# A convolution's pair sums put between the scans and the next gates, and the start of the recurrence gate written in another order

## The chip, the cores and the metric

The kernel runs on one core of a Trainium2 chip. The metric is the device time of one execution in microseconds (us), the median of three runs. Five engines work side by side, each through a queue of its own in a fixed order: TensorE (PE, matmuls), VectorE (DVE), ScalarE (ACT), GpSimd (POOL) and SyncE (SP, which here issues DMA transfers). An instruction waits until what it reads is written and what it overwrites has been read.

## The reference, cut to what matters

Two layers over 1024 latent tokens of 1024 channels (and 256 context tokens that feed the recurrence alone). The change lies in the first layer:

```python
z = h @ p["w_in"]
va, vg, ga, xb, gb = jnp.split(z, [...], axis=-1)
# branch A: 31 taps along the tokens, then layernorm
u = va * jax.nn.sigmoid(vg)
u = depthwise_conv(u, p["conv_w"], p["conv_b"], CONV_PAD)
y_a = jax.nn.silu(layernorm(u, p["ln_g"], p["ln_b"])) * jax.nn.silu(ga)
# branch B: a gated linear recurrence, forwards and backwards
a, bx = lru_coeffs(u2, p)         # u2: 4 taps over xb; sigmoid gates from 128 x 128 blocks
y_b = (scan forwards + scan backwards) * jax.nn.silu(gb)
x = x + gate[:, None] * (jnp.concatenate([y_a, y_b], axis=-1) @ p["w_out"])
```

Everything is float32. A product is formed in three matmuls (high by high, high by low, low by high) from operands that are split into a high part (a cast, names ending in h) and the remainder (a subtraction, names ending in l).

## The kernel before

Channels lie on the 128 partitions, so that a tile holds 128 channels and 1024 tokens, and each of the first layer's products is done in 8 column blocks j. A loop of **8 rounds** (L661 to L740) goes through the blocks. In round j, PE forms vg, va, the context's and the latents' xb of the next block, and the gates of this block, 12 groups of three matmuls dealt out between those of xb (`gate_steps`, L630). ACT turns the gate groups into sigmoids; POOL subtracts the low parts of the weights (`wl_vg`, `wl_va`, `wl_xb`) and multiplies the recurrence's inputs (`rec_input`, `rec_scaled`: tiles `l` with `uc`, and `l` with `l`); DVE does the four taps (`uc`), the products va by sigmoid (`u`), and for the block before it the two directions' scans (`rec_scan`, L610) and their sum (`rec_sum`, L624: tile `l`, 128 x 1024, both operands in SBUF).

The 31-tap convolution (`conv`, L509) is a stream of small DVE steps that `fill(n)` draws into the other work, n steps at a time: the numbers of `fill` set how far each conv has come at each place. It works on even and odd tokens apart: one sum over even taps, one over odd taps, and one of both phases' sum with summed taps, from which the others are subtracted. That sum is formed in place, odd tokens plus even tokens (L528, tile `u`, two SBUF operands). Most steps accumulate in PSUM (tile `conv`) and so have one SBUF operand. At a conv's end, L547 adds its result to the layernorm's sum (`lnsum`).

In the rounds and up to L926 the helpers `on`, `act`, `cast`, `gp`, `vec` (L441 to L497) hold each engine to the order of the code. `fixed[0] = False` (L928) frees DVE's; from there a scheduler orders the work.

The gate of branch B is multiplied in a loop after the rounds (L910): for each block, the weights of a gb product, the product, its silu (`sb`), and `yr` (the scans' sum, read back from DRAM, times the silu) with its split (`ybh`, `ybl`). The products `wob` of L951 read these. The layernorm follows on its sum: `mu` (L936) is a matmul with ones over `lnsum`, and the products `ga` (L995) wait in PSUM until the normalised `u` is multiplied in (L1001).

The eight gate columns of the modulation (L655, a sum over a product of a loaded tile `l` with the condition's tile `cL`) stand ahead of the rounds; `cL` isn't used afterwards.

Of the kernel before, what the change touches and what calls it, by code (L numbers as in the profile page):

```python
# [55 lines left out]
def body(ctx, tc, xT, ctxT, cc, ccol, modT, modW, win, gw, wout, wu, grp, wg, wo1, small, edge, ident, outT):  # L56
# [443 lines left out]
    def tap(acc_, src, w, o, last_=False):  # L500
        a, b = max(0, -o), H - max(0, o)
        vec(nc.vector.scalar_tensor_tensor, out=(src if last_ else acc_)[:, a:b], in0=src[:, a + o : b + o],
            scalar=w, in1=acc_[:, a:b], op0=mult, op1=add)
        if last_:
            vec(nc.vector.tensor_copy, out=src[:, b:], in_=acc_[:, b:])
# [3 lines left out]
    def conv(j):  # L509
        acc_, late = banks(f"conv{j}", 0)  # L510
        ue, uo = us[j][:, 0::2], us[j][:, 1::2]
        bias, edge_ = col(O_CONVB + j), edges[:, j : j + 1]
# [17 lines left out]
        tap(acc_, ue, w(2 * NT - 1), NT - 1 - 7, True)  # L530
        yield
        vec(nc.vector.scalar_tensor_tensor, out=acc_, in0=uo, scalar=both(7), in1=ue, op0=mult, op1=sub)
# [3 lines left out]
        vec(nc.vector.scalar_tensor_tensor, out=late[:, : H - 1], in0=uo[:, 1:], scalar=both(8), in1=late[:, 1:],  # L536
            op0=mult, op1=sub)
        vec(nc.vector.tensor_copy, out=late[:, H - 1 :], in_=edge_)
        yield
        for i, n in enumerate([n for n in range(NT) if n not in (7, 8)]):  # L540
            tap((acc_, late)[i % 2], uo, both(n), n - 7)
            yield
        tap(acc_, uo, both(NT), NT - 7, True)
# [3 lines left out]
        for h in range(2):  # L547
            if j > 0:
                first = us[0][:, HALF[h]] if j == 1 else lnacc[h][:, :H]
                vec(nc.vector.tensor_tensor, out=lnacc[h][:, :H], in0=first, in1=us[j][:, HALF[h]], op=add)  # L550
                yield
# [15 lines left out]
    with ExitStack() as actx:  # L567
# [87 lines left out]
        for m in range(2 * KT, 3 * KT):  # L655
            raw = L[m % 6][:, :D]
            nc.sync.dma_start(raw, modT[0, m])
            mod_tile(m0, 0, m, raw, (cL,), raw)

        state, free = None, [L[0], L[1], L[2], L[3], L[4], L[5]]  # L660
        for j in range(KT):  # L661
# [15 lines left out]
            if state is None:  # L677
                act(sg[1], vg[1], AF.Sigmoid)
            uh, ul = utile(f"uh{j}", F32R), utile(f"ul{j}", F32R)
            cast(uh, uc)  # L680
            if state is not None:
                act(sg[1], vg[1], AF.Sigmoid)
# [48 lines left out]
            for n, _ in enumerate(gate_steps(j, (gwh, gwl), (uh, ul), gates)):  # L731
# [3 lines left out]
                if n == 7:  # L735
# [3 lines left out]
            fill(5)  # L739
# [12 lines left out]
        def gb_product(j, w):  # L752
            gps[j] = [psum(f"gb{j}_{h}") for h in range(2)]
# [156 lines left out]
    for j in range(1, KT + 1):  # L910
        if 1 < j < KT:
            gb_silu(j)
        gb_weights(j + 2)
        if j + 2 < KT:
            gb_product(j + 2, gws[j + 2])
        n = j - 1
        th, tl = d2tile(f"ybh{n}", F32R), d2tile(f"ybl{n}", F32R)
        for h in range(2):
# [5 lines left out]
            fill(6)  # L924
        bh.append(th)
        bl.append(tl)  # L926

    fixed[0] = False  # L928
    all_of(going[0])
    for j in range(begun[0], KT):  # L930
        all_of(conv(j))

# [662 lines left out]
```

## Time and profile before

| | |
|---|---|
| median of 3 runs (lowest, highest) | 1392.46 us (1392.46, 1395.89) |
| the profiled execution's own time | 1395.02 us |
| its span, first to last instruction | 1393.2 us |
| mean granted TensorE clock | 0.971 |
| busy DVE, ACT, POOL | 1204.9, 627.7, 353.0 us |

The span is what one execution's instructions take; the run's own time has 1.8 us around it. A busy share is an average over stages with different limits. The stages of interest lie between 100 and 700 us: the modulation's gate columns and the first round (to 150), the rounds (to 467), the recurrence gate's products (to 582), the `wob` products (to 657), and the layernorm with the `ga` products. Times in rows count from the span's start. In a row of the timeline stand the start, the length, engine, line, operation, names (output, arrow, inputs), shapes, a count, and in brackets the idle time of the engine before it with what ended it.

### The profile page before, as it was taken

Reading aid. Unit: us, or ns where it says so; the run is one execution under the profiler, and the core shown is the slowest. Engines: PE = TensorE matmul, PEld = TensorE weight load, DVE = VectorE, ACT = ScalarE, POOL = GpSimd, SP = SyncE. Lnnn points to the kernel's source line nnn. Section 1 sums busy time; section 2 is a strip of 40 time slices with the busy share of each in tenths; the row PEclk is TensorE's granted clock in tenths of the full one; section 3 lists DMA queues with packets and bytes.
Section 4 is the critical chain, followed back from the end, with each engine's and each line's share of the span. In section 5 each row is a group of like instructions: output and inputs, shape, how many; then the busy total and the mean of one; then the engine's idle time right before and its main releaser. Section 6 shows DMA issues by size and latency. Waiting matters only on the chain. (4 is left out here: it accounts for less than half of the span.)

```text
span 1393.2 us, 15819 instructions
## 1 busy us (share of the span) xinstructions
PE 1293.3 (93%) x5664; PEld 1046.3 (75%) x5664; DVE 1204.9 (86%) x1790; ACT 627.7 (45%) x902; POOL 353.0 (25%) x172
## 2 busy tenths in 40 slices
PE   7888999999899959899699999999999999899896
PEld 5467887887787848688488788788878888778684
DVE  7986699999999999988887884999989986876775
ACT  6352656664556613201643544753333434534442
POOL 5182454464536525412411004100000000000002
PEclk9999999999999989999899999999999999999998
DMA  9744111111112122253244635523334324757633
GB/s 349 279 136 159 38 45 39 69 68 38 61 53 69 46 76 98 96 177 129 75 151 139 211 132 198 169 70 136 133 124 137 121 97 145 242 187 265 231 110 121
DMA packets 82866, 181.79 MB, mean 130 GB/s; under 512 B 7778, under 2 KB 27618, under 8 KB 82788
## 3 DMA queue, kind: packets, MB, share of 16 engines
q1 hardware_dynamic: 74340, 176.60, 36.7%
q10 hardware_dynamic: 8448, 4.20, 1.0%
q8 instruction: 44, 0.72, 0.2%
q14 instruction: 34, 0.28, 0.1%
HBM read 136.72 MB, written 44.04 MB: 130 GB/s over the span
## 5 line engine op out<-in xcount | busy, mean ns | idle before, releaser
L445 DVE SCALAR_TENSOR_TENSOR conv<-u,sm,conv 128x505 f32<-128x505 f32 (+6 forms) x196 | 134.1, 742 | 0.8
L1415 POOL TENSOR_TENSOR o<-x,rr 128x256 f32<-128x256 f32 (+1 forms) x9 | 8.0, 930 | 462.6 <-ACT rr L1403 460.0
L445 ACT ACTIVATE l<-g,sm 128x512 f32<-128x512 f32 (+1 forms) x96 | 58.0, 617 | 79.0 <-PE g L445 59.6
L103 POOL TENSOR_TENSOR wl_wu<-wr_wu,wh_wu 128x1024 fp32r<-128x1024 f32 x16 | 39.8, 2491 | 153.6 <-ACT wh_wu L102 148.1
L133 PE MATMUL ga<-h0h,wh_ga 128*128 128x512 f32 x128 | 50.9, 398 | 13.5 <-DVE u L1001 13.5
L445 PE MATMUL gb<-h0h,wh_gb 128*128 128x512 f32 x128 | 51.0, 399 | 12.1 <-ACT wh_gb L445 12.1
L445 POOL TENSOR_TENSOR l<-l,uc 128x1280 f32<-128x1280 f32 x16 | 61.9, 3891 | 0.0
L445 DVE SCALAR_TENSOR_TENSOR conv<-u,wsum,conv 128x506 f32<-128x506 f32 (+3 forms) x88 | 60.2, 743 | 0.2
L445 DVE TENSOR_TENSOR_SCAN l<-l,l 128x256 f32<-128x256 f32 (+1 forms) x32 | 56.5, 1767 | 1.1
L256 PE MATMUL fold<-gh,wh_wu 128*128 128x512 f32 x128 | 52.8, 414 | 3.1 <-ACT wh_wu L102 3.1
L257 PE MATMUL fold<-gl,wh_wu 128*128 128x512 f32 x128 | 52.1, 407 | 3.7 <-DVE gl L103 3.7
L445 POOL TENSOR_TENSOR l<-l,l 128x1280 f32<-128x1280 f32 x16 | 47.8, 3010 | 27.0 <-ACT l L445 22.8
L258 PE MATMUL fold<-gh,wl_wu 128*128 128x512 f32 x128 | 51.5, 411 | 3.4 <-POOL wl_wu L103 3.4
L445 PE MATMUL gb<-h0h,wl_gb 128*128 128x512 f32 x128 | 50.9, 398 | 3.2 <-POOL wl_gb L445 3.2
L133 PE MATMUL wob<-ybh,wh_wob 128*128 128x512 f32 x128 | 51.0, 404 | 3.0 <-ACT ybh L445 2.3
L134 PE MATMUL wob<-ybl,wh_wob 128*128 128x512 f32 x128 | 51.8, 404 | 0.6 <-POOL ybl L445 0.6
L135 PE MATMUL wob<-ybh,wl_wob 128*128 128x512 f32 x128 | 51.9, 406 | 0.0
L135 PE MATMUL ga<-h0h,wl_ga 128*128 128x512 f32 x128 | 51.0, 399 | 0.0
L134 PE MATMUL ga<-h0l,wh_ga 128*128 128x512 f32 x128 | 50.8, 397 | 0.0
L445 PE MATMUL gb<-h0l,wh_gb 128*128 128x512 f32 x128 | 50.8, 397 | 0.0
L445 PE MATMUL va<-h0h,wl_va 128*128 128x512 f32 x128 | 50.0, 391 | 0.0
L445 PE MATMUL va<-h0l,wh_va 128*128 128x512 f32 x128 | 49.8, 389 | 0.0
(583 smaller groups left out, 4381.3 us busy)
## 6 DMA issues: line engine op xcount, KB each, us to landing
mod<-modT SPq DMA_DIRECT2D x20, 512.0 KB, 6.7
wr_wu<-wu SPq DMA_DIRECT2D x16, 512.0 KB, 4.0
x_part<-xp SPq DMA_DIRECT2D x32, 256.0 KB, 2.3
mod<-modT SPq DMA_DIRECT2D x32, 256.0 KB, 3.2
wr_v<-wfold SPq DMA_DIRECT2D x16, 512.0 KB, 4.0
wr_g<-wg SPq DMA_DIRECT2D x16, 512.0 KB, 5.5
wr_wo<-wo SPq DMA_DIRECT2D x16, 512.0 KB, 4.3
yr_t<-y_t SPq DMA_DIRECT2D x16, 512.0 KB, 5.8
```

Source lines behind the costliest of these rows:

```text
L103: eng.tensor_tensor(out=lo, in0=src, in1=hi.bitcast(F32), op=sub))
L133: nc.tensor.matmul(ps, hi[:, kc], xh[k][:, cols], start=(k == 0), stop=False)
L134: nc.tensor.matmul(ps, hi[:, kc], xl[k][:, cols], start=False, stop=False)
L135: nc.tensor.matmul(ps, lo[:, kc], xh[k][:, cols], start=False, stop=(k == ks - 1))
L256: nc.tensor.matmul(ps, wh[:, kc], gh[i], start=(i == 0), stop=False)
L257: nc.tensor.matmul(ps, wh[:, kc], gl[i], start=False, stop=False)
L258: nc.tensor.matmul(ps, wl[:, kc], gh[i], start=False, stop=(i == 3))
L445: last[eng] = f(*args, **kw)
L1415: nc.gpsimd.tensor_tensor(out=o[:, k - k0], in0=v, in1=rr, op=mult)
```

## The change

- `conv` of blocks 0 to 4 no longer forms the two phases' sum in place. `spread_sum` writes it to a half of `cL`, and the later steps read it there. Blocks 5 to 7 keep the old form.
- `at_rest`, right after `rec_sum` in a round, forms these sums for blocks that are ready (`spread_sum`) and adds ended convs to the layernorm's sum (`ln_sums`, which counts no longer as a step of `conv`).
- In a round the cast and subtraction of the next vg's weights and the first `rec_input` go from behind the gate group 7 to behind group 9 (L735; the last round keeps 7).
- The numbers of `fill` change: 10 for 9, 3 for 4, 4 for 5 in a round, 19 for 5 at the first round's end, 22 for 24 after the rounds. A conv has 49 or 50 steps; before it had 50, and two more for the layernorm's sum from block 1 on.
- The modulation's gate columns move into the first round, behind DVE's `ul`, with one addition for all eight; in that round ACT casts `uh` ahead of the second sigmoid.
- The recurrence gate: the weights and the product of block 3 go ahead of the last scans, block 4's weights right behind them, and its product to the wide PSUM tile. The first two blocks' `yr` stand together with 2 steps of conv between halves; the others keep 6.

```diff
-        vec(nc.vector.tensor_tensor, out=uo, in0=uo, in1=ue, op=add)
+        if ub is uo:
+            vec(nc.vector.tensor_tensor, out=uo, in0=uo, in1=ue, op=add)
+            yield
+        tap(acc_, ue, w(2 * NT - 1), NT - 1 - 7, ue)
...
+    def ln_sums():
+        for j in range(summed[0], ended[0]):
+            for h in range(2):
                 first = us[0][:, HALF[h]] if j == 1 else lnacc[h][:, :H]
                 vec(nc.vector.tensor_tensor, out=lnacc[h][:, :H], in0=first, in1=us[j][:, HALF[h]], op=add)
+        summed[0] = max(summed[0], ended[0])
+
+    def spread_sum():
+        j = spread_[0]
+        vec(nc.vector.tensor_tensor, out=cL[:, HALF[j % 2]], in0=us[j][:, 1::2], in1=us[j][:, 0::2], op=add)
+        spread_[0] += 1
...
+    def at_rest():
+        ln_sums()
+        while spread_[0] < min(whole_[0], ended[0] + 2, NSPREAD):
+            spread_sum()
...
-        for m in range(2 * KT, 3 * KT):
-            raw = L[m % 6][:, :D]
-            nc.sync.dma_start(raw, modT[0, m])
-            mod_tile(m0, 0, m, raw, (cL,), raw)
...
+            if state is None:
+                for m in range(2 * KT, 3 * KT):
+                    part = L[m % 6][:, :D]
+                    nc.sync.dma_start(part, modT[0, m])
+                    vec(nc.vector.scalar_tensor_tensor, out=part, in0=part, scalar=1.0, in1=cL,
+                        op0=mult, op1=mult, accum_out=m0[:, 0, m : m + 1])
+                vec(nc.vector.tensor_tensor, out=m0[:, 0, 2 * KT :], in0=m0[:, 0, 2 * KT :],
+                    in1=col(O_MB + 2 * KT, KT), op=add)
...
-                fill((9, 6)[h])
+                fill((10, 6)[h])
...
-            fill(4)
+            fill(3)
...
                 rec_sum(state)
+            at_rest()
...
-                if n == 7:
+                if n == (7 if final else 9):
                     w = raw_split(raw, name)
                     rec_input(now, 0)
             all_of(steps)
-            fill(5)
+            fill(19 if state is None else 4)
...
-            gps[j] = [psum(f"gb{j}_{h}") for h in range(2)]
+            if j == 4:
+                gps[j] = (lambda t: [t[:, h] for h in HALF])(wide(f"gb{j}"))
+            else:
+                gps[j] = [psum(f"gb{j}_{h}") for h in range(2)]
...
+        gb_weights(3)
         gb_silu(0)
         gb_silu(1)
-        fill(24)
+        gb_product(3, gws[3])
+        fill(22)
         for d in range(2):
             rec_scan(state, d)
         rec_sum(state)
+        at_rest()
+        gb_weights(4)
...
+    for j in range(2, KT + 1):
+        if 2 < j < KT:
+            gb_silu(j)
+        if j > 2:
+            gb_weights(j + 2)
+        if j + 2 < KT:
+            gb_product(j + 2, gws[j + 2])
+        if j == 2:
+            gated(0, 2)
+            gb_silu(2)
+        gated(j - 1, 2 if j == 2 else 6)
+        ln_sums()
```

`gated(n, between)` is the old body of the loop for one block: two halves of `yr`, each followed by its split and `fill(between)`.

Where the rows stand on the engines. First DVE around the first scans (round 1). `l` rows are the recurrence's: a multiplication, a scan over the context (128x256) and one over the latents (128x1024) for each direction (the listing names scans SCALAR_TENSOR_TENSOR too), then the sum of both. Before:

```order
L445 SCALAR_TENSOR_TENSOR l_832<-l_831,l_832 128x1280
L445 SCALAR_TENSOR_TENSOR l_832<-l_831,l_832 128x256
L445 SCALAR_TENSOR_TENSOR l_832<-l_831,l_832 128x1024
L445 TENSOR_TENSOR l_830<-l_830,l_832 128x1024
L445 SCALAR_TENSOR_TENSOR conv_0_1112<-u_1030,wsum,conv_0_1112 128x505
L445 SCALAR_TENSOR_TENSOR conv_1_1113<-u_1030,wsum,conv_1_1113 128x506
```

The same place in the changed kernel:

```order
L445 SCALAR_TENSOR_TENSOR l_832<-l_831,l_832 128x1280
L445 SCALAR_TENSOR_TENSOR l_832<-l_831,l_832 128x256
L445 SCALAR_TENSOR_TENSOR l_832<-l_831,l_832 128x1024
L445 TENSOR_TENSOR l_830<-l_830,l_832 128x1024
L445 TENSOR_TENSOR cL<-u_1343 128x512
L445 SCALAR_TENSOR_TENSOR u_1023<-u_1023,sm,conv_1_1106 128x512
L445 TENSOR_SCALAR conv_0_1575<-u_1343,sm 128x512
```

The phases' sum of the next block (`cL`) now follows the recurrence's sum, and the conv has come further: its first block ends here.

Second, ACT after the rounds, where gb weights are cast and `yr` is split. `sb` are the silus, `ybh` the cast of `yr`. Before:

```order
L445 ACTIVATE sb_0_3644<-gb_0_3523 128x512
L445 ACTIVATE sb_1_3645<-gb_1_3524 128x512
L445 CAST wh_gb_3699<-wr_gb_3697 128x1024
L445 CAST ybh_3753<-yr_0_3755 128x512
L232 ACTIVATE cH<-cH 128x512
L445 CAST ybh_3753<-yr_1_3767 128x512
L445 ACTIVATE sb_0_3780<-gb_0_3586 128x512
L445 ACTIVATE sb_1_3781<-gb_1_3587 128x512
L445 CAST wh_gb_3786<-wr_gb_3784 128x1024
```

The same place in the changed kernel:

```order
L445 CAST wh_gb_3655<-wr_gb_3653 128x1024
L445 ACT_TABLE_LOAD
L445 ACTIVATE sb_0_3659<-gb_3417 128x512
L445 ACTIVATE sb_1_3660<-gb_3417 128x512
L445 ACTIVATE sb_0_3663<-gb_0_3536 128x512
L445 ACTIVATE sb_1_3664<-gb_1_3537 128x512
L445 CAST wh_gb_3754<-wr_gb_3752 128x1024
L445 CAST ybh_3821<-yr_0_3823 128x512
```

The fourth product's weights (block 4: 3786 before, 3754 now) no longer stand behind the first `ybh` casts, and block 3's (3699 before, 3655 now) stand ahead of the silus.

Third, PE at the layernorm's sum, near the end of the `wob` products (`mu` reads `lnsum`; the first and second half are two matmuls). Before, with rows of the last product's both halves:

```order
L135 MATMUL wob_0_4808<-ybh_4190,wl_wob_4805 128x512
L133 MATMUL wob_1_4837<-ybh_3753,wh_wob_4804 128x512
L134 MATMUL wob_1_4837<-ybl_3754,wh_wob_4804 128x512
L936 MATMUL mu_4323<-lnsum_822,ones 128x512
L135 MATMUL wob_1_4837<-ybh_3753,wl_wob_4805 128x512
```

In the changed kernel:

```order
L133 MATMUL wob_0_4800<-ybh_3841,wh_wob_4796 128x512
L977 MATMUL mu_0_4282<-lnsum_821,ones 128x512
L134 MATMUL wob_0_4800<-ybl_3842,wh_wob_4796 128x512
L977 MATMUL mu_4315<-lnsum_822,ones 128x512
L135 MATMUL wob_0_4800<-ybh_3841,wl_wob_4797 128x512
```

The first `mu` stood at place 2582 of PE's 5574 rows, in the last block of the product's first half; it stands at 2563 now, in that half's second block, and the layernorm's two later matmuls keep their distance from it to within a few rows (92 for the first).

More of the change, by code (lines that the diff above doesn't have):

```diff
@@ L497, in vec, with tap @@
         return on("vec", f, **kw) if fixed[0] else f(**kw)
-    def tap(acc_, src, w, o, last_=False):
+    def tap(acc_, src, w, o, dst=None):
         a, b = max(0, -o), H - max(0, o)
-        vec(nc.vector.scalar_tensor_tensor, out=(src if last_ else acc_)[:, a:b], in0=src[:, a + o : b + o],
+        vec(nc.vector.scalar_tensor_tensor, out=(acc_ if dst is None else dst)[:, a:b], in0=src[:, a + o : b + o],
             scalar=w, in1=acc_[:, a:b], op0=mult, op1=add)
-        if last_:
-            vec(nc.vector.tensor_copy, out=src[:, b:], in_=acc_[:, b:])
+        if dst is not None:
+            vec(nc.vector.tensor_copy, out=dst[:, b:], in_=acc_[:, b:])
     def conv(j):
@@ L535, in conv @@
         yield
-        vec(nc.vector.scalar_tensor_tensor, out=late[:, : H - 1], in0=uo[:, 1:], scalar=both(8), in1=late[:, 1:],
+        vec(nc.vector.scalar_tensor_tensor, out=late[:, : H - 1], in0=ub[:, 1:], scalar=both(8), in1=late[:, 1:],
             op0=mult, op1=sub)
@@ L540, in conv @@
         for i, n in enumerate([n for n in range(NT) if n not in (7, 8)]):
-            tap((acc_, late)[i % 2], uo, both(n), n - 7)
+            tap((acc_, late)[i % 2], ub, both(n), n - 7)
             yield
-        tap(acc_, uo, both(NT), NT - 7, True)
+        tap(acc_, ub, both(NT), NT - 7, uo)
         yield
@@ L546, in conv, with both_sum @@
         yield
-        for h in range(2):
-            if j > 0:
+        ended[0] = j + 1
+    ended, summed, spread_ = [0], [1], [0]
+    NSPREAD = 5
+    def ln_sums():
+        for j in range(summed[0], ended[0]):
+            for h in range(2):
                 first = us[0][:, HALF[h]] if j == 1 else lnacc[h][:, :H]
                 vec(nc.vector.tensor_tensor, out=lnacc[h][:, :H], in0=first, in1=us[j][:, HALF[h]], op=add)
-                yield
+        summed[0] = max(summed[0], ended[0])
[3 more added lines that the diff above has]
+        spread_[0] += 1
+    def both_sum(j):
+        while spread_[0] <= j:
+            spread_sum()
+        return cL[:, HALF[j % 2]]
+    def at_rest():
+        ln_sums()
+        while spread_[0] < min(whole_[0], ended[0] + 2, NSPREAD):
+            spread_sum()
     going, begun, whole_ = [iter(())], [0], [0]
@@ L676, in body @@
             all_of(mm3_fixed(vg[1], w, (hh, hl), HALF[1]))
-            if state is None:
-                act(sg[1], vg[1], AF.Sigmoid)
             uh, ul = utile(f"uh{j}", F32R), utile(f"ul{j}", F32R)
             cast(uh, uc)
-            if state is not None:
-                act(sg[1], vg[1], AF.Sigmoid)
+            act(sg[1], vg[1], AF.Sigmoid)
             fill(2)
@@ L909, in body, with gated @@
     bh, bl = [], []
[L910 to L916, printed above, removed]
+    def gated(n, between):
         th, tl = d2tile(f"ybh{n}", F32R), d2tile(f"ybl{n}", F32R)
@@ L923, in body @@
             gp(out=tl[:, HALF[h]], in0=y, in1=th[:, HALF[h]].bitcast(F32), op=sub)
-            fill(6)
+            fill(between)
         bh.append(th)
         bl.append(tl)
+    for j in range(2, KT + 1):
[10 more added lines that the diff above has]
+        ln_sums()
     fixed[0] = False
     all_of(going[0])
+    ln_sums()
     for j in range(begun[0], KT):
         all_of(conv(j))
+        ln_sums()
     for h in range(2):
```

5 lines of the change are left out of this document (2 added, 3 removed).

## The prediction

> **What bounds the kernel now.** I read the busy times first, then the waits of the busiest engine, then the stages one by one, and last the rows around each place of the change.
>
> ```profile
> PE 1293.3 (93%) x5664; PEld 1046.3 (75%) x5664; DVE 1204.9 (86%) x1790; ACT 627.7 (45%) x902; POOL 353.0 (25%) x172
> ```
>
> PE is busiest, but the change takes no matmul away; it can only shorten PE's waits. The waits of PE between 100 and 700 us (total, times, longest):
>
> ```profile
> PE ga L133 <- DVE u L1001: 13.5, 1, 13.5
> PE gb L445 <- ACT wh_gb L445: 12.1, 1, 12.1
> PE g L445 <- DVE u L445: 9.3, 6, 5.0
> PE gb L445 <- POOL wl_gb L445: 3.2, 3, 1.7
> PE xbc L445 <- ACT wh_xb L445: 3.2, 1, 3.2
> PE wob L133 <- ACT ybh L445: 2.3, 1, 2.3
> PE xbc L445 <- POOL wl_xb L445: 2.3, 1, 2.3
> PE g L445 <- DVE uc L445: 1.3, 2, 0.7
> PE wob L133 <- DVE xp L959: 0.7, 1, 0.7
> PE wob L134 <- POOL ybl L445: 0.6, 1, 0.6
> ```
>
> Together 48.5 us. The stages (length, then busy time of PE, PEld, DVE, ACT and POOL, granted clock):
>
> ```profile
> 126.00:140.00 14.00, 8.55 (x40) 7.51 (x40) 8.68 (x15) 3.66 (x5) 3.95 (x2) 0.76 0.24 76
> 200.00:467.00 267.00, 256.37 (x1198) 212.26 (x1198) 264.17 (x296) 156.08 (x179) 138.25 (x49) 0.99 0.16 56
> 467.00:582.00 115.00, 99.70 (x425) 80.83 (x424) 113.67 (x155) 38.34 (x51) 51.77 (x27) 0.94 0.25 86
> 582.00:657.00 75.00, 71.38 (x290) 56.59 (x289) 65.54 (x104) 10.52 (x13) 18.26 (x8) 0.93 0.46 154
> ```
>
> From 200 to 582 DVE is busy 99% of the time and PE is not: **DVE sets the pace there**, and PE waits for it directly (`u`, `uc`) or through ACT. A wait of PE also costs clock:
>
> ```profile
> 360.30:367.10 6.80, 4.34 (x11) 3.51 (x12) 6.73 (x11) 0.69 (x1) 0.60 (x1) 0.50 0.01 2
> 515.00:520.00 5.00, 3.73 (x10) 2.55 (x9) 5.00 (x7) 0.62 (x1) 3.00 (x2) 0.50 0.41 143
> 586.00:596.00 10.00, 9.26 (x21) 6.48 (x22) 8.77 (x15) 1.99 (x2) 4.73 (x3) 0.51 0.65 193
> ```
>
> After the waits of 5.0, 12.1 and 2.3 us the clock is half for some microseconds; half of the time that PE is busy at it is lost: 2.2, about 3 and 4.5 us, and at the start (126 to 140, clock 0.76) 2.4 us.
>
> **What DVE loses.** Its groups with two SBUF operands, and the rows of one undisturbed and two disturbed cases:
>
> ```profile
> L445 DVE TENSOR_TENSOR_SCAN l<-l,l 128x1024 f32<-128x1024 f32 x16 | 45.5, 2842 | 0.6
> L445 DVE TENSOR_TENSOR l<-l,l 128x1024 f32<-128x1024 f32 x8 | 26.1, 3266 | 0.3
> L445 DVE TENSOR_TENSOR u<-u 128x512 f32<-128x512 f32 x7 | 14.0, 1994 | 0.2
> L445 DVE TENSOR_TENSOR lnsum<-lnsum,u 128x512 f32<-128x512 f32 x8 | 10.4, 1342 | 0.1
> ...
> 504.20 1.22 DVE L445 TENSOR_TENSOR l<-l,l 128x1024 f32<-128x1024 f32 x1
> 481.15 0.69 DVE L445 TENSOR_TENSOR u<-u 128x512 f32<-128x512 f32 x1
> 237.05 3.08 DVE L445 TENSOR_TENSOR_SCAN l<-l,l 128x256 f32<-128x256 f32 x2
> 240.16 3.24 DVE L445 TENSOR_TENSOR l<-l,l 128x1024 f32<-128x1024 f32 x1
> 238.40 3.92 POOL L445 TENSOR_TENSOR wl_vg<-wr_vg,wh_vg 128x1024 fp32r<-128x1024 f32 x1 [10.21 <-DVE l L445]
> 193.94 5.03 DVE L445 TENSOR_TENSOR_SCAN l<-l,l 128x256 f32<-128x256 f32 x2
> 199.00 3.79 DVE L445 TENSOR_TENSOR l<-l,l 128x1024 f32<-128x1024 f32 x1
> 194.37 2.45 POOL L445 TENSOR_TENSOR wl_vg<-wr_vg,wh_vg 128x1024 fp32r<-128x1024 f32 x1 [12.35 <-DVE l L445]
> ```
>
> The recurrence's sum takes 1.22 us with POOL idle and 3.2 to 3.8 beside POOL, a pair of scans 3.08 or 5.03, a 512-wide sum 0.69 or more. Against these undisturbed times the groups lose 8 x (3.27 - 1.22) = 16.4, four scans x 1.95 = 7.8, 7 x (1.99 - 0.69) = 9.1 and 8 x (1.34 - 0.69) = 5.2 us: 38.5 us of DVE, about 30 of them between 200 and 467. The rows also say how: `wl_vg` of 238.40 takes 3.92 instead of 2.45, as if it stood still until the scan's end at 240.13, and the sum of 240.16 as if it stood until `wl_vg` ended. The Trainium skill, "SBUF — State Buffer", section "Who interferes with whom", states such a lock: one engine holds the shared port for its whole instruction, and the other fully blocks. By it a sum that begins behind `wl_vg` here would pay up to 2.45 us more, which is the second rival below; a sum begun first would pay nothing.
>
> **The change, part by part** (against the profiled execution, span 1393.2).
>
> *First round.* Now `uh` waits for DVE's taps, which stand between the modulation's products:
>
> ```profile
> 128.49 1.26 ACT L445 CAST uh<-uc 128x1280 fp32r<-128x1280 f32 x1 [11.14 <-DVE m L223]
> ```
>
> With these eight products (10 us) behind `ul`, `uh` and after it `wh_xb` and `wl_xb` come about 10 us earlier, and PE's waits of 3.2 + 2.3 us go, with 2.4 us of clock: **-7.9**. Next late are the products `u`, which move from 131 to about 130, behind the eight products: just in time, since the gates need the PSUM of va at about 131 once xbc no longer waits. The eight loads keep their place on SP's queue, two of them later; the gates write the tiles `l` only after 130, by when the products are done. If that cover failed, each further product would cost PE 1.2 us. The 14 more steps of conv at this round's end (19 for 5) fill a DVE wait of 12.4 us that stands there now.
>
> *Rounds.* POOL's `wl_vg` now follows gate group 9, which overwrites what the last scan reads; so neither scan meets it, and the recurrence's sum of 1.22 us ends before the sigmoid (0.48) and the cast (1.04) let POOL begin:
>
> ```profile
> 239.72 0.48 ACT L445 ACTIVATE l<-g,sm 128x256 f32<-128x256 f32 x1 [0.86 <-PE g L445]
> 237.23 1.04 ACT L445 CAST wh_vg<-wr_vg 128x1024 fp32r<-128x1024 f32 x1
> 199.61 0.39 PE L445 MATMUL vg<-h0h,wl_vg 128*128 128x512 f32 x1
> 199.83 0.39 PE L445 MATMUL vg<-h0h,wh_vg 128*128 128x512 f32 x1
> ```
>
> DVE's need in 200 to 467 falls from 264 by about 30, and by one step of conv per round (0.7), and rises by four phases' sums: about 234 us. PE's own need is 256.4 less 2.2 of clock. So PE becomes the pace here, with some 3 us of slack per round for DVE; its waits of 9.3 + 1.3 and 2.2 of clock go, 12.8 us. What stays disturbed (the conv's steps of two SBUF operands outside the stretch, and a `wl_va` that comes later and meets `ul`) is not in the trace in this position. It is between 0 and one blocked operation of 2 to 2.5 us in each of 7 rounds, and I leave 4 us of PE's waits, as most of it falls into the slack: **-8.8**. The new place of the cast costs nothing if the scan ends early enough: from gate 9's sigmoid at 239.72, 0.48 + 1.04 + 2.45 us end at about 243.8, and PE needs the low part at about 244. Behind the cast on ACT stand only two sigmoids; behind `wl_vg` on POOL two products that DVE needs half a round later.
>
> *From the last round to the layernorm.* Here DVE has this to do until `mu` can run:
>
> ```profile
> 470.61 10.44 DVE L445 SCALAR_TENSOR_TENSOR conv<-u,sm,conv 128x510 f32<-128x510 f32 x15
> 651.96 1.02 PE L936 MATMUL mu<-lnsum,ones 128*128 128x512 f32 x2
> 653.02 2.48 DVE L939 TENSOR_TENSOR u<-u,mu 128x512 f32<-128x512 f32 x4 [4.72 <-PE mu L936]
> ```
>
> Counting steps without the layernorm's sums: before, 400 in all, of them 215 drawn by the last recurrence sum of the rounds; now 395 and 228. That leaves 185 before and 167 now, 18 fewer at 10.44 / 15 = 0.7 us: -12.5. That last round's scans and sum are undisturbed: -4.5. And DVE waits 4.7 us before 653 because PE reached `mu` late in its queue; it stands 19 places earlier, at 0.22 us each (the step from 199.61 to 199.83 above): -4.2, of which I take 3.5. DVE's way is shorter by **-20.5**. PE's own way to `mu` loses the 12.1 + 3.2 and about 3 of clock, because block 3's product and block 4's weights no longer stand behind `yr` (now ACT's cast of block 4 is free when block 2's product ends), and the 19 places: about -22. The later of the two sets `mu`, so -20.5 stands; the waits at `wob` stay, as `ybh` comes from DVE.
>
> *After `mu`* the chain to the `ga` wait's end is unchanged, 44.6 us:
>
> ```profile
> 696.58 0.80 PE L133 MATMUL ga<-h0h,wh_ga 128*128 128x512 f32 x1 [13.53 <-DVE u L1001]
> ```
>
> The wait stays near 12 us. From there on PE's and DVE's work is as before: 0.
>
> Sum: -7.9 - 8.8 - 20.5 = **-37.2 us**. The profiled execution took 1395.02, the median of the runs shown is 1392.46; I take the difference off the median: 1355.
>
> One rule speaks on the clock. The wait of 2.3 us at `wob`, with two of 0.7 and 0.6 behind it, was followed by 10 us at 0.51. The Trainium skill, "TensorE: Matmul & The Clock Gate", Part 1, gives an idle window of about 3.4 us as what throttles; by it such short waits would be free of it, and the residue in the rounds would be 4 us flat. The measurement differs, so shorter waits may cost double.
>
> **Rivals.**
> 1. *PE goes through.* DVE is ready everywhere before PE, so all of PE's waits up to `mu` go (35 us), the clock losses (12) and the 19 places: -51, about **1341**. For it: DVE's slack in the rounds. Against it: DVE has 167 steps left after the rounds, and fixed `fill` numbers let it not work ahead.
> 2. *The change does half of what it says*: sums of the stretch still meet POOL, because two layernorm sums and a phases' sum after 1.22 us outlast the 1.5 us to `wl_vg`. Three of the rounds have such sums; blocked sums and a blocked `ul` at 2 to 2.5 us each in seven rounds give back 15 to 25: **1370 to 1380**.
> 3. *Slower: PE waits for `wl_vg` every round.* If DVE's last scan ends late, as at 198.97 against PE's first low vg matmul at 199.61, the sigmoid, the cast and 2.45 us put the low part about 3 us late, and with half clock behind it (2 to 4 us) each of 7 rounds costs about 6.3: +44, against 28 gained elsewhere: **1408**. It turns slower from about 4 us per round. Against it: it needs scans that stay as late although DVE's work shrinks.
>
> **How the numbers follow.** Forecast 0.52 (1347 to 1363), rival 1 0.17, rival 2 0.24, rival 3 0.04, and 0.03 for a wash of several. The range reaches into both first rivals: 1340 to 1378. Faster by over 0.3% (4.2 us, about what a measurement of this kernel can tell from no change): 0.93; within it 0.03; slower 0.04.
>
> **What would show it.** Right: the recurrence's sum near 1.2 us in all 8 rounds and all scan pairs near 3.1; no wait of `xbc`; the wait for `wh_gb` gone; PE over 98% busy in the rounds; `mu` near 615. Wrong: a new group of waits of vg on POOL's `wl_vg` (rival 3), `cL` or `lnsum` sums of 2 us and more (rival 2), a `ga` wait well under 10 us (rival 1), or `mu` reached by PE long before DVE is ready, with half clock behind it.

## The result, and the profile after

The changed kernel takes 1351.47 us (median of four runs, 1348.80 to 1356.63) beside 1393.90 of the kernel before on the same chip: a ratio of 0.9699, with a 95% interval of 0.9663 to 0.9735. The prediction was 1355 in a range of 1340 to 1378. The profiled execution took 1349.46 us, its span is 1347.7 (before: 1393.2), so 45.5 us less in the traces and 42.4 in the medians.

The busy times, and the waits of PE between 100 and 660 us (total, times, longest):

```profile
PE 1280.7 (95%) x5664; PEld 1040.2 (77%) x5664; DVE 1171.6 (87%) x1783; ACT 629.9 (47%) x902; POOL 338.1 (25%) x172
...
PE ga L133 <- DVE u L1042: 8.7, 1, 8.7
PE wob L133 <- ACT ybh L445: 2.7, 3, 1.3
PE gb L445 <- ACT wh_gb L445: 2.6, 1, 2.6
PE gb L445 <- POOL wl_gb L445: 1.7, 1, 1.7
PE wob L133 <- DVE xp L1000: 0.8, 1, 0.8
PE g L445 <- DVE u L445: 0.8, 1, 0.8
PE wob L134 <- POOL ybl L445: 0.6, 1, 0.6
```

17.9 us in place of 48.5 (`xp` is DVE's step that adds a finished `wob` product to x). Nothing waits for `xbc` any more, and the one wait of `g` that is left stands at 131 us, in the first round. The stages (length, busy time of PE, PEld, DVE, ACT and POOL, granted clock):

```profile
126.00:140.00 14.00, 13.20 (x74) 11.24 (x73) 13.86 (x26) 4.17 (x7) 0.00 (x0) 1.00 0.11 40
190.00:450.00 260.00, 260.00 (x1237) 218.79 (x1236) 241.85 (x307) 163.93 (x185) 131.88 (x52) 1.00 0.16 57
450.00:555.00 105.00, 97.37 (x405) 77.46 (x403) 102.07 (x140) 34.65 (x48) 47.42 (x27) 0.95 0.27 96
555.00:615.00 60.00, 59.19 (x258) 48.25 (x258) 54.42 (x86) 7.64 (x9) 15.77 (x7) 1.00 0.50 171
```

In the rounds the two engines have changed places: PE is busy 260 of 260 us, at full clock, and DVE 241.85. From 450 to 555 DVE is the fuller one still (97%), and from 555 to `mu` PE is again. DVE's groups that answer to those of before:

```profile
L445 DVE TENSOR_TENSOR_SCAN l<-l,l 128x1024 f32<-128x1024 f32 x16 | 37.6, 2351 | 0.6
L445 DVE SCALAR_TENSOR_TENSOR l<-l,l 128x1280 f32<-128x1280 f32 x16 | 27.0, 1690 | 0.0
L445 DVE TENSOR_TENSOR l<-l,l 128x1024 f32<-128x1024 f32 x8 | 11.8, 1476 | 0.3
L445 DVE TENSOR_TENSOR lnsum<-lnsum,u 128x512 f32<-128x512 f32 x8 | 6.2, 819 | 0.0
L445 DVE TENSOR_TENSOR cL<-u 128x512 f32<-128x512 f32 x5 | 3.4, 686 | 0.0
```

The scans fell from 45.5 to 37.6 us, the recurrence's sums from 26.1 to 11.8, and the phases' sums in their new tile take 0.69 us each. The products `yr`, which have two SBUF operands too, fell from 17.3 to 14.5. One row stands against the change: the operation that opens a scan (`l<-l,l` of 128x1280) took 23.6 us before. Its extra 3.4 us are two rows at the last scans, and beside them stands the one recurrence sum that still meets POOL:

```profile
439.93 3.23 DVE L445 TENSOR_TENSOR l<-l,l 128x1024 f32<-128x1024 f32 x1
462.04 2.77 DVE L445 SCALAR_TENSOR_TENSOR l<-l,l 128x1280 f32<-128x1280 f32 x1
467.84 3.62 DVE L445 SCALAR_TENSOR_TENSOR l<-l,l 128x1280 f32<-128x1280 f32 x1
474.60 1.23 DVE L445 TENSOR_TENSOR l<-l,l 128x1024 f32<-128x1024 f32 x1
```

### The profile page after: what moved, and what is told of

Its sections match the earlier page's. It is cut to its first block, busy times and chain, and to the rows that moved or that the text cites. A ratio compares the mean times of both kernels' runs of the same rounds, so it can differ in the third digit from the quotient of the medians.

```text
span 1347.7 us, 15827 instructions
## 1 busy us (share of the span) xinstructions
PE 1280.7 (95%) x5664; PEld 1040.2 (77%) x5664; DVE 1171.6 (87%) x1783; ACT 629.9 (47%) x902; POOL 338.1 (25%) x172
## 5 line engine op out<-in xcount | busy, mean ns | idle before, releaser
L445 POOL TENSOR_TENSOR l<-l,l 128x1280 f32<-128x1280 f32 x16 | 47.0, 2961 | 28.5 <-ACT l L445 14.4
L102 ACT CAST wq_wo<-wr_wo 128x512 fp32r<-128x512 f32 x48 | 28.8, 618 | 48.2 <-DMA wr_wo<-wo 18.5
L445 PE MATMUL vg<-h0l,wh_vg 128*128 128x512 f32 x128 | 49.8, 389 | 0.0
L445 PE MATMUL vg<-h0h,wh_vg 128*128 128x512 f32 x128 | 49.8, 389 | 0.0
L445 PE MATMUL vg<-h0h,wl_vg 128*128 128x512 f32 x128 | 49.8, 389 | 0.0
L445 PE MATMUL va<-h0h,wh_va 128*128 128x512 f32 x128 | 49.8, 389 | 0.0
```

What stands on the lines that cost most here:

```text
L102: return (nc.scalar.copy(hi, src), eng.tensor_tensor(out=lo, in0=src, in1=hi.bitcast(F32), op=sub))
L445: last[eng] = f(*args, **kw)
```

## The experiments

Differences below are those of the ratios to the kernel before on the same chip, times 1393.9; the intervals reach 0.1 to 0.4% (2 to 6 us) to either side. So the time alone tells a kernel from the changed one only beyond some 6 to 8 us; for the smaller differences the traces have to speak. A place in a trace also carries a little that is not the edit's: the first product `u` of the first round starts at 130.94 us in the changed kernel and at 132.44 with two steps more.

| kernel | median us | ratio to before | against the changed kernel |
|---|---|---|---|
| changed | 1351.47 | 0.9699 (0.9663 to 0.9735) | |
| cast after 7 | 1370.98 | 0.9829 (0.9801 to 0.9856) | +18.1 |
| sums in conv | 1363.47 | 0.9775 (0.9740 to 0.9810) | +10.6 |
| modulation ahead | 1359.41 | 0.9758 (0.9724 to 0.9791) | +8.2 |
| gate as before | 1352.36 | 0.9695 (0.9653 to 0.9738) | -0.6 |
| before, cast after 9 | 1385.59 | 0.9954 (0.9929 to 0.9979) | |
| before, new gate | 1393.82 | 1.0005 (0.9977 to 1.0032) | |
| last scans apart | 1351.88 | 0.9716 (0.9688 to 0.9745) | +2.4 |
| one step more | 1344.41 | 0.9661 (0.9638 to 0.9685) | -5.3 |
| two steps more | 1356.68 | 0.9729 (0.9706 to 0.9752) | +4.2 |
| four steps more | 1391.52 | 0.9984 (0.9970 to 0.9998) | +39.7 |
| cast after 10 | 1368.18 | 0.9801 (0.9771 to 0.9831) | +14.2 |
| several together | 1351.52 | 0.9692 (0.9672 to 0.9711) | -1.0 |

### One part undone at a time

**The cast after gate group 7 again.**

```diff
-                if n == (7 if final else 9):
+                if n == 7:
```

> The changed kernel, but the low part of vg's weights is made after gate group 7 again in all rounds, not after 9. Theory (POOL's subtraction blocks DVE's operations of two SBUF operands): the recurrence's sums go from 1.22 to 3 us or more in 6 or 7 rounds, about half of the scan pairs from 3.08 to about 5; DVE needs 2 to 3 us more per round against 0.8 us of waiting in it, so PE waits 1.2 to 2.2 us in each of seven rounds, with some half clock behind: 1359 to 1371 us, wl_vg itself no longer than 4 us. Rival (the gain comes from the other edits, the place of the cast is hidden): within 3 us of 1351.5, PE's waits in the rounds below 3 us in all.

The line moves the first `rec_input` along with the cast and the subtraction, as the change did; they were not separated. Measured: 1370.98, at the upper end of the theory. DVE's groups of this kernel:

```profile
L445 DVE TENSOR_TENSOR_SCAN l<-l,l 128x1024 f32<-128x1024 f32 x16 | 39.6, 2474 | 0.6
L445 DVE TENSOR_TENSOR l<-l,l 128x1024 f32<-128x1024 f32 x8 | 16.4, 2049 | 0.3
L445 DVE TENSOR_TENSOR lnsum<-lnsum,u 128x512 f32<-128x512 f32 x8 | 14.0, 1785 | 0.0
L445 DVE TENSOR_TENSOR cL<-u 128x512 f32<-128x512 f32 x5 | 9.0, 1792 | 0.0
L445 DVE TENSOR_TENSOR lnsum<-u,u 128x512 f32<-128x512 f32 x2 | 6.3, 3166 | 0.0
```

The size was right and the way was not. Three recurrence sums and two scans met POOL, not six or seven, and one of the three is the last round's, which meets POOL in the changed kernel too; mostly it was the layernorm's and the phases' sums, which the change had put behind them. And PE waited in few rounds: 6.9 us in four waits of `g`, 4.0 of them in one. Most of DVE's lag did not show in the rounds at all but came due behind them: the gate's first product starts 6.6 us later than in the changed kernel (432.2 against 425.6), the last recurrence sum 14.4 us later (489.0 against 474.6).

**The sums in the convolution again.**

```diff
-    NSPREAD = 5
+    NSPREAD = 0
...
         yield
-        ended[0] = j + 1
+        for h in range(2):
+            if j > 0:
+                first = us[0][:, HALF[h]] if j == 1 else lnacc[h][:, :H]
+                vec(nc.vector.tensor_tensor, out=lnacc[h][:, :H], in0=first, in1=us[j][:, HALF[h]], op=add)
+                yield
```

> The changed kernel, but the phases' sums (in place) and the layernorm's sums stand in the convolution again, each as a step of its own; the fill numbers stay. Theory: about 14 to 16 of the 228 steps drawn by the end of the last round are now sums, so as many steps of 0.7 us are left over behind it (+10 us on DVE's way to mu, of which PE's own way there hides about 3), and a sum meets POOL here and there (0.6 to 1.3 us each); the rounds keep PE's pace: 1357 to 1364 us. Rival 1 (only the meetings with POOL count): +1 to +4 us. Rival 2 (the rounds too fall back behind DVE): 1365 us or more, with PE's waits for u in the rounds.

Measured: 1363.47, as the theory had it. The rounds keep PE's pace (length, then busy time of PE, PEld and DVE):

```profile
200.00:430.00 230.00, 230.00 (x1101) 193.85 (x1100) 217.44 (x269) 145.16 (x163) 113.02 (x44) 1.00 0.19 60
```

The gate starts at 426.2 us, about where it does in the changed kernel (425.6); `mu` runs at 623.4 in place of 610.9. So what this part gave was the room behind the rounds. The longest waits of PE there (`ms_ln` is the layernorm's second matmul, over the squares that follow `mu`):

```profile
PE ga L133 <- DVE u L1046: 14.5, 1, 14.5
PE ms_ln L188 <- POOL lnsum L991: 3.9, 1, 3.9
PE wob L133 <- DVE xp L1004: 3.8, 2, 2.9
```

**The modulation's products ahead of the rounds again**, with the sigmoid ahead of `uh` in the first round:

```diff
         other_taps(0, xc, uc[:, :C])
+        for m in range(2 * KT, 3 * KT):
+            raw = L[m % 6][:, :D]
+            nc.sync.dma_start(raw, modT[0, m])
+            mod_tile(m0, 0, m, raw, (cL,), raw)
...
-            if state is None:
-                for m in range(2 * KT, 3 * KT):
...
```

> The changed kernel, but the modulation's eight gate products stand before the rounds again, ahead of uh. Theory (the first term, 7.9 us, is a wait of PE that nothing later hides): PE waits 3 and 2 us for wh_xb and wl_xb before 140 us with half clock behind, and 1358 to 1361 us. Rival (PE runs ahead of DVE later on and gives it back): 1351 to 1355 us, with the ga wait shorter by as much as the start is longer.

Measured: 1359.41, and the two waits are back (3.2 us for `wh_xb`, 2.0 for `wl_xb`), while the `ga` wait is 8.7 as in the changed kernel: nothing gave it back.

**The gate's beginning as before.**

```diff
-        gb_weights(3)
         gb_silu(0)
         gb_silu(1)
-        gb_product(3, gws[3])
-        fill(22)
+        fill(24)
...
         at_rest()
-        gb_weights(4)
...
-    for j in range(2, KT + 1):
+    for j in range(1, KT + 1):
...
-        gated(j - 1, 2 if j == 2 else 6)
+        gated(j - 1, 6)
```

> The changed kernel, but the gate of the recurrence branch begins as before (block 3's product and block 4's weights behind the gated tiles of block 0, 24 steps of fill at one place), the rest as changed. Theory (PE's own way to mu was as long as DVE's): the waits of 12 and 2 us for wh_gb and wl_gb come back with 2 to 4 us of half clock, mu stands 19 places later (4 us), DVE's way is as in the changed kernel and ends 3 us ahead of PE's: +14 to +20 us, 1365 to 1372 us. Rival (DVE alone sets mu, and the gate's order is hidden behind it): within 4 us of 1351.5, with the wait for wh_gb back but mu no later than 615.

Measured: 1352.36; the theory fell and the rival's time held. The longest of PE's waits:

```profile
PE gb L445 <- ACT wh_gb L445: 7.1, 1, 7.1
PE wob L133 <- ACT ybh L445: 3.8, 2, 2.4
PE gb L445 <- POOL wl_gb L445: 1.3, 1, 1.3
```

The wait for `wh_gb` is longer again, and the wait for `u` at `ga` (8.7 us) is gone: `mu` runs 8.4 us earlier than in the changed kernel (602.45 against 610.86), because DVE's last scans are undisturbed (1.49 and 1.47 us for the operations that took 2.77 and 3.62), it waits for no load of `yr` (2.0 us in the changed kernel) and less at `xp` (0.8 for 4.1). So the rival's reason holds only in part: the order is not hidden behind DVE, it costs DVE as much as it saves PE.

### One part alone in the kernel of before

```diff
-                if n == 7:
+                if n == (7 if final else 9):
```

> The kernel before, with only the cast of vg's weights moved from behind gate group 7 to behind 9 (not in the last round). Theory (POOL's subtraction no longer meets the scans and the recurrence's sum; PE becomes the pace of the rounds): sums at 1.22 us in six or seven rounds, PE's waits for u and uc (9.3 + 1.3 us) and 2.2 us of half clock gone, the first round and the part behind the last round as before: 10 to 14 us faster, 1379 to 1384 us. Rival (the place of the cast is worth as much alone as it cost when it alone was undone, 19.5 us, since DVE carries its gain on to mu): 1372 to 1376 us.

Measured: 1385.59, 0.46% faster (0.21 to 0.71%), some 6 us and less than either had. The rounds end 7.7 us earlier (`gb` from 438.6 us, before 446.3), but one round still pays a wait of 3.0 us at 352.9. The recurrence's sum is at 1.2 us in five rounds of eight, not in six or seven. In the round of the wait two layernorm sums in the convolution meet POOL's products (DVE's row, then POOL's):

```profile
349.96 4.62 DVE L445 TENSOR_TENSOR lnsum<-lnsum,u 128x512 f32<-128x512 f32 x2
```

```profile
347.71 6.31 POOL L445 TENSOR_TENSOR l<-l,l 128x1280 f32<-128x1280 f32 x2 [3.18 <-ACT l L445]
```

Undisturbed the two would take 1.4 us. The cast takes POOL away from the scans, but not from these sums. That they must leave the convolution for that is not shown: with the sums left in it, but the other edits in place, PE waited in no later round (above). What else in the change the rounds need, the numbers of `fill` before all, stays open.

The new beginning of the gate alone (the opposite of the last diff above, in the kernel before):

> The kernel before, with only the new beginning of the gate. Theory (DVE sets mu; what PE saves at the gate it waits later, and the two weight subtractions on POOL now meet the last scans): the waits for wh_gb and wl_gb fall from 15 to 5 us or less, the last scans' first operations go from 1.47 to about 3 us, and the time is within 4 us of before, 1389 to 1397 us. Rival (PE's 12 us wait with its half clock is on the path): 1376 to 1382 us.

Measured: 1393.82, no change. PE's waits:

```profile
PE ga L133 <- DVE u L1013: 11.7, 1, 11.7
...
PE ms_ln L188 <- POOL lnsum L958: 7.5, 1, 7.5
PE gb L445 <- ACT wh_gb L445: 4.3, 1, 4.3
```

The 12.1 us of `wh_gb` became 4.3, and 7.5 us of waiting for the layernorm's own sum appeared. `mu` runs at 652.4 us, before at 652.0: DVE sets it. The expected disturbance of the last scans did not occur here (the mean of their first operations is 1475 ns); its place hangs on where DVE stands when POOL starts.

### Less on DVE's way behind the rounds

**The last scans apart from POOL's subtractions:**

```diff
-        fill(22)
-        for d in range(2):
-            rec_scan(state, d)
+        fill(24)
+        rec_scan(state, 0)
+        fill(3)
+        rec_scan(state, 1)
```

> The changed kernel, with five steps of the convolution moved to the last scans: two ahead of the first (fill of 24 for 22), three between the two, so that POOL's subtractions for gate blocks 3 and 4 fall beside steps with a PSUM operand. Theory (these two meetings cost DVE 3.4 us on its way to mu): the scans' first operations at 1.5 us in place of 2.77 and 3.62, mu and the end of the ga wait 3 to 4 us earlier, 1347 to 1349 us. Rival (DVE's way has slack there, or PE sets mu): within 1 us of the changed kernel.

Measured: 1351.88, a miss; by the ratio the kernel is no faster. The edit did what it should: the two operations take 1.48 and 1.69 us, and `mu` runs at 606.27, 4.6 us earlier. But the `ga` wait ends only 2.0 us earlier (653.00 against 655.00). DVE's rows on the way there are the first reciprocal of the layernorm's roots (`sq_ln`) and the second group of products with it. First of the changed kernel, then of this one:

```profile
636.14 3.35 DVE L191 RECIPROCAL lnsum<-sq_ln 128x512 f32<-128x512 f32 x1 [4.11 <-ACT sq_ln L190]
649.07 5.28 DVE L1027 TENSOR_TENSOR u<-u,lnsum 128x512 f32<-128x512 f32 x8
```

```profile
632.09 3.35 DVE L191 RECIPROCAL lnsum<-sq_ln 128x512 f32<-128x512 f32 x1 [6.58 <-ACT sq_ln L190]
645.28 7.06 DVE L1028 TENSOR_TENSOR u<-u,lnsum 128x512 f32<-128x512 f32 x8
```

2.5 us more are waited at the first, but it still stands 4.05 us earlier. Most of the rest is lost in the second group, which takes 1.8 us more: one product beside POOL's `wl_ga` takes 2.84 us for 0.68. And the half clock behind the `ga` wait lasted 10.2 us in place of 6.8. The spans are equal (1347.9 and 1347.7).

**One step of the convolution more in each round:**

```diff
-                fill((10, 6)[h])
+                fill((11, 6)[h])
```

> The changed kernel with one more step of the convolution in each round (fill of 11 for 10 ahead of the first product u). Theory (PE is the pace of the rounds and DVE waits 0.7 to 0.9 us in each; behind them DVE sets mu): a round stays at 42.5 us, 7 steps of 0.7 us fewer are left behind the rounds, and the time falls by 4 to 5 us, to 1346 to 1348. Rival 1 (DVE's slack in a round is not at that place): PE waits 0.5 to 0.7 us in each round and the time is within 1 us of the changed kernel. Rival 2 (waits with half clock behind them): 1353 us or more.

Measured: 1344.41, and each of its four runs (1343.61 to 1348.09) is below each of the changed kernel's, though the kernel before ran 1.6 us lower beside it too (1392.30 for 1393.90); the intervals of the ratios overlap (0.9638 to 0.9685, 0.9663 to 0.9735). The rounds, first of the changed kernel, then of this one:

```profile
200.00:430.00 230.00, 230.00 (x1102) 193.86 (x1101) 214.23 (x278) 145.19 (x163) 110.39 (x44) 1.00 0.16 58
```

```profile
200.00:430.00 230.00, 230.00 (x1100) 193.81 (x1100) 221.76 (x288) 145.27 (x163) 110.88 (x44) 1.00 0.18 58
```

PE goes through as before, DVE does 7.5 us more in the same time, the `ga` wait falls to 5.1 us and ends at 647.93.

**Two, and four, steps more:**

```diff
-                fill((10, 6)[h])
+                fill((11, 6)[h])
...
-            fill(3)
+            fill(4)
```

> The changed kernel with two more steps of the convolution in each round (fills of 11 for 10 and 4 for 3). Theory (DVE waits 15.8 us in 200 to 430 of the changed kernel, 2.9 us per round, and one added step still left 1.5 of them): rounds stay at 42.5 us without a wait of PE, mu 4 to 5 us earlier than with one step, the ga wait of 5.1 us falls to 0 to 1: 1339 to 1342 us. Rival (the slack lies elsewhere in the round than the second step): PE waits for u or uc in most rounds, and the time is that of one added step, 1344 us, or more.

> The changed kernel with four more steps in each round (fills of 12 for 10 and 5 for 3). Theory: four steps are 2.8 us, all of DVE's slack of 2.5 to 2.9 us per round, so PE begins to wait for u or uc by some tenths in some rounds; and mu gains nothing more once the ga wait is gone, since PE then goes through: 1339 to 1345 us, no better than with two steps by over 1 us. Rival 1 (the end still depends on DVE): another 8 to 10 us faster than with two steps, below 1334. Rival 2 (DVE is the pace again in every round): 1346 us or more.

Four steps are fills of 12 and 5. Measured: 1356.68 and 1391.52, both worse than the theory allowed, and the second within 4 us of the kernel before. With two steps PE still waits in no round after the first, as foreseen (DVE is busy 224.13 of 230 us), but DVE stands 6.6 us later at the end of the last round and meets POOL: its sum there takes 3.79 us (3.23 in the changed kernel), with a disturbed scan of 4.31 ahead, and the last recurrence sum starts at 481.7 in place of 474.6. PE then waits 6.0 us for `wh_gb` and 5.7 for `xp`. With four steps all of it is back; PE's waits:

```profile
PE g L445 <- DVE u L445: 12.8, 5, 7.3
PE gb L445 <- ACT wh_gb L445: 10.3, 1, 10.3
PE vg L445 <- POOL wl_vg L445: 5.6, 4, 1.8
PE xbc L445 <- POOL wl_xb L445: 4.8, 2, 2.4
PE g L445 <- POOL wl_gw L445: 3.0, 1, 3.0
```

The recurrence's sums take 3.2 us in five rounds again and 3.79 in the last, and 2.1 and 2.2 us are the means of the sums in the stretch (`cL`, `lnsum`). The work is the same as in the changed kernel; only its place differs, by 2.8 us per round.

### The cast one gate group later

```diff
-                if n == (7 if final else 9):
+                if n == (7 if final else 10):
```

> The changed kernel with the cast of vg's weights one gate group later, after 10. Theory (the cast after 9 is just in time: wl_vg ends at 233.61 in the round of 218, and PE's first matmul with it starts at 234.00): wl_vg comes about 1.4 us later, PE waits about 1 us for it in each of seven rounds, without half clock behind so short a wait: 1356 to 1361 us, with a group of seven waits of vg for wl_vg of 6 to 8 us in all. Rival (there is slack of more than 1.4 us behind the cast): within 2 us of the changed kernel. Rival 2 (each wait costs half clock too): 1370 us or more.

In the changed kernel the low part is ready 0.39 us ahead of its first use (POOL's row, then PE's):

```profile
231.19 2.42 POOL L445 TENSOR_TENSOR wl_vg<-wr_vg,wh_vg 128x1024 fp32r<-128x1024 f32 x1 [14.35 <-DVE u L445]
```

```profile
234.00 0.39 PE L445 MATMUL vg<-h0h,wl_vg 128*128 128x512 f32 x1
```

One group later, PE and DVE's `ul` show:

```profile
PE vg L445 <- POOL wl_vg L445: 7.3, 7, 1.1
```

```profile
L445 DVE TENSOR_TENSOR ul<-uc,uh 128x1280 fp32r<-128x1280 f32 x8 | 17.4, 2178 | 3.4 <-ACT uh L445 3.4
```

The waits are as foreseen, seven of 1.05 us, none with half clock behind it. The time, 1368.18, is more than expected. The span is 18.3 us longer, the waits are 7.3 of them; the gate starts 10.0 us later (435.6), and another 5 come up to `mu` (625.58). `ul` takes 2178 ns in place of 1485, so it now meets POOL's `wl_va`, 5.5 us of DVE in all, and half clock lasts 10.2 us at two places behind the rounds (6.8 and 3.4 in the changed kernel). How the other 11 us divide between these wasn't taken apart.

### Several together

One step more per round, the last scans apart, gate block 5's weights ahead of block 1's gated tiles, and fills of 5 for 6 between the later ones:

```diff
-                fill((10, 6)[h])
+                fill((11, 6)[h])
...
+            gb_weights(5)
-        gated(j - 1, 2 if j == 2 else 6)
+        gated(j - 1, 2 if j == 2 else 5)
```

> The changed kernel with one more step per round (fill of 11), the five steps at the last scans (two ahead, three between), the weights of gate block 5 ahead of block 1's gated tiles, and fills of 5 for 6 between the later gated tiles. Theory (behind the rounds DVE's way to mu and on to the ga wait sets the end, and a wait that PE is spared ahead of mu it waits at ga): against one more step alone (1344.4) mu comes 3 to 5 us earlier by the undisturbed scans, the ga wait's end 2 to 4 us earlier, the waits at gb and wob (6.8 us in all) mostly go without counting: 1340 to 1344 us. Rival 1 (PE's spared waits count in full): 1335 to 1339 us. Rival 2 (another meeting of DVE and POOL takes the gain): 1345 us or more.

Measured: 1351.52, a miss, 4 us over one step alone by the ratios. The last scans are undisturbed, as meant: the operations that open a scan have a mean of 1515 ns, with one step alone 1728, 3.4 us over the sixteen. But the products `yr` take as much more, first with one step alone, then here:

```profile
L445 DVE TENSOR_TENSOR yr<-yr,sb 128x512 f32<-128x512 f32 x16 | 13.9, 871 | 3.4 <-DMA yr<-yb_raw 2.7 <-POOL ybl L445 0.7
```

```profile
L445 DVE TENSOR_TENSOR yr<-yr,sb 128x512 f32<-128x512 f32 x16 | 17.5, 1094 | 2.7 <-DMA yr<-yb_raw 2.7
```

Three of them take 2.2 to 2.4 us for 0.68, each beside a POOL subtraction for the next weights (`wl_gb`, `wl_wob`). That is the meeting of the second rival, at another place than the scans. DVE's waits from 480 to 612 us:

```profile
DVE xp L1002 <- PE wob L135: 4.2, 6, 1.0
DVE u L982 <- PE mu L979: 3.5, 1, 3.5
DVE yr L445 <- DMA yr<-yb_raw: 2.7, 3, 1.5
```

DVE also waits for PE now, at the evictions `xp` and at `mu`, whose places between the other work are fixed in each engine's queue; and the wait at `sq_ln` is 6.6 us here too. Neither one step more alone (871 ns) nor the last scans apart alone (906) has the long `yr`; whether gate block 5's weights, the fills of 5 or the combination bring them stays open. The lowest ratio of all is that of one step more, though not clear of this one by the intervals.

## Why the prediction was right, and where it was not

The time fell inside the range and the main cause is the one foreseen. By the traces the gain is 8.3 us larger than the 37.2 of the sum; 4.2 of these stand in the rounds and 3.9 behind the `ga` wait. By the prediction's own steps:

- **What bounds the kernel.** DVE set the pace of the rounds because its operations of two SBUF operands met POOL's; with these apart, PE sets it. Shown: the cast after 7 brings long sums back, and four steps more bring them back with the whole of the old time. The slack of "some 3 us per round" was 230 - 214.23 = 15.8 us in 5.4 rounds of 42.5, which is 2.9. The Trainium skill, "SBUF — State Buffer", section "Who interferes with whom", has one engine hold the shared port for a whole instruction, and the prediction made 2.45 us of it for a sum that begins behind `wl_vg`. The trace agrees: the first layernorm sums with the cast after 7 take 3.17 us in the mean for 0.69, 2.5 more. The first of them begins 0.10 us behind `wl_vg`; the second meets the product that POOL does next.
- **First round, -7.9.** Undone, it cost 8.2 us; the clock from 126 to 140 is 1.00 for 0.76. Right.
- **Rounds, -8.8.** From the first product `va` of the second round (167.2 and 159.5 us) to the gate's start (446.3 and 425.6) the kernels take 279.1 and 266.1: -13.0. The 12.8 us of waits and clock were right; the step that failed is the residue of 4 us left on them, which measured nothing. `wl_va` does not meet `ul` (1485 ns, 1483 before), and what the convolution still loses fits into the slack. One group later `ul` did meet it (2178 ns). The cast alone gave 7.7 us here, so the other edits have a share too, but the place of the sums is not what the rounds need: with them back in the convolution the gate starts at 426.2 us. Which other edit it is isn't shown.
- **The cast "just in time".** Right, with 0.39 us of margin. The slower rival's wait appeared when the cast moved by one group, in each of seven rounds, but without the half clock that the rival had put behind it. With four steps more it appeared too, in four rounds (5.6 us in all).
- **From the last round to `mu`, -20.5.** From the gate's start to `mu` it is 205.7 us before (446.3 to 652.0) and 185.3 after: -20.4. The sum was right and its parts were not; that it came out to 0.1 us is luck. Putting the sums back cost 10.6 us, near the 12.5 of the 18 steps. The "-4.5" of an undisturbed last round was too much: the cast stays behind 7 there, so the sum still takes 3.23 us (3.79 before), the scan pair 3.08 (5.04), 2.5 us together. Two things no term had: the gate's new order disturbs the last scans by 3.4 us, and the products `yr` meet POOL less, by 2.8. DVE's wait for `mu` fell from 4.7 to 1.0 us, but 2.6 of them only moved to the `xp` ahead of it. That DVE, not PE, sets `mu` was right: the gate's order, worth 12.1 + 3.2 us of PE's waits, is worth nothing in either kernel; in the changed one DVE comes to `mu` 8.4 us later with it.
- **After `mu`, 0, with the wait "near 12".** The chain is 44.1 us, nearly as before (610.86 to 655.00; 44.6). The wait is 8.7, not near 12: the same 19 places that bring `mu` forward leave PE more of the `wob` products to do behind it, by the forecast's own step 19 x 0.22 = 4.2 us, and 13.5 - 4.2 is 9.3. The half clock behind it was 6.8 us for 13.7, and 3.4 for 6.8 behind the next wait; from the end of the `ga` wait on the kernel takes 692.7 us, before 696.6. So the term of 0 for this stretch was mis-sized by 3.9.
- **Rivals.** PE going through (1341) came halfway: in the rounds yes, behind them no; its sign, a `ga` wait under 10 us, appeared. Stretch sums meeting POOL did not occur in the rounds of the change (all at 0.69 us or less); cast after 7 shows them (the sums at 1.8 us, +18.1). Of the signs of being right, two came short: one recurrence sum of eight is not near 1.2 us, and the wait for `wh_gb` fell to 2.6 us but did not go.

Of the 42.0 us that 1 - 0.9699 stands for, the four parts undone one by one account for 18.1 + 10.6 + 8.2 - 0.6 = 36.3; the rest is within their intervals, or belongs to the fill numbers, which weren't undone alone. Nor need the parts add up: the cast is worth 18.1 us undone and 6.4 alone.

## What to carry to other kernels

Where two engines block each other, look at when they meet before looking at how long each operation takes: the same work in other places was worth 40 us here, and a schedule with 2.9 us of slack and 0.39 us of margin per round falls back as a whole when a few steps are added. A wait of the busiest engine is worth removing only if no other engine is as late at the next point where they join; undoing that one part alone tells. Fill the slack by one step at a time, and look at each stage behind it again.

## What the runs showed of the hardware

The clock's records in all traces run at half speed for 3.4 us or a multiple of it (3.4, 6.8, 10.2, 13.7, up to 23.9; only the last stretch, at the end of the span, fits none), and the same wait of 8.69 us at `ga` was followed by 6.8 us in the changed kernel and by 10.2 with the cast after 7. A lone wait of 1.0 to 1.5 us had no half clock behind it (seven of 1.05 with the cast after 10). Two or three close together had it sometimes: 1.07 and 1.71 us within 3.5 us at the gate, with one step more, were followed by 3.4 us at half. The Trainium skill, "TensorE: Matmul & The Clock Gate", Part 1, describes a free-running window of about 3.4 us; the multiples agree, and so does the free lone wait, which the prediction doubted. An idle time of a whole window was not needed here: in the kernel before the wait of 2.3 us at `wob`, with two of 0.6 and 0.7 behind it, had 10.2 us at half clock behind it.

A scan (2.35 us, up to 4.31), the operation that opens it (1.47, up to 3.62) and a product of eight columns in the convolution (`edge_junk`, 0.16 us where undisturbed, mean 919 ns over seven in the changed kernel) all wait for POOL as the plain sums do. This breadth was not expected; so each of DVE's operations with two SBUF operands has to be placed, also the smallest.
